# Bonus sums in column groups, later turns, and joined runs of small matmuls in a decoder layer on one core

## The chip, the cores and the metric

The kernel runs on one core of one Trainium2 chip. The metric is device time in microseconds of one execution. The kernel before takes 408.7 us, the median of three runs (408.42 to 409.23).

## What is computed

One decoder layer on 256 tokens of 1024 channels, all in float32. Two branches mix tokens from the same normalised input: RWKV-7 (a recurrence over time with a 64x64 state for each of 8 heads) and softmax attention (8 heads of 64, causal; with 256 tokens there is one key block, so the block choice picks nothing more). Both are gated and merged, projected, added to the input, and followed by a gated MLP with a short convolution. Cut to what the change touches:

```python
def step(state, inp):
    r_t, w_t, k_t, v_t, a_t, b_t = inp
    sa = jnp.einsum('bhvk,bhk->bhv', state, a_t)
    state = (state * w_t[:, :, None, :] + sa[..., None] * b_t[:, :, None, :]
             + v_t[..., None] * k_t[:, :, None, :])
    return state, jnp.einsum('bhvk,bhk->bhv', state, r_t)
...
y = ((y - mu) * lax.rsqrt(var + GN_EPS)).reshape(B, S, C)
y = y * ln_g.astype(f32) + ln_b.astype(f32)
bonus = (jnp.sum(rh * kh * r_k.astype(f32), axis=-1, keepdims=True) * vh).reshape(B, S, C)
return ((y + bonus) * g.astype(f32)).astype(z.dtype)
```

The bonus needs, for each token and head, one sum over the head's 64 channels, and that sum again at each of the 64 channels.

## The kernel before

**Projections.** Weights come from HBM in pieces of 512 KB (`load_next`, on SyncE's queue), are split by ScalarE into a high half (`split_hi`, L262) and by VectorE into a low half (`split_lo`, L272), and each product is made of three matmuls: high by high, high by low, low by high. `wst` (L300 to L305) makes blocks of 12 matmuls with 256 columns, `xst` (L321 to L325) blocks of 6 with 512 columns. These projections are the bulk of TensorE's work. The two first blocks are written out by hand in `first_steps` (L469 to L484): the first piece, its two halves (`first(0, ...)`), then the second (`first(1, ...)`), whose low half GpSimd makes (L459). Between the two stand `params_turned` (L146, a transpose of 43 rows of small parameters) and `late_params` (L150 to L152, three VectorE instructions which copy the result and derive two more vectors). Behind them comes `tl` (L490), a product with four column groups. In `first_steps` the order of every engine but SyncE is the written one (`manual_schedule`).

**The recurrence** is cut into four chunks of 64 tokens (`chain`). Within a chunk it is a triangular system. Its 64x64 matrices are inverted in levels: 16x16 blocks on the diagonal by VectorE (L722 to L750), which reach it and leave it through DRAM (`d1`, `Tb`, `d2`, `d3`, then `X0` and `X`, L695 to L772), and then two levels of small matmuls on TensorE. The first level has three products: `pp` (L836, into `P`), `px` (L850, back into `X0`) and `pxt` (L864, into `X`). `pp` and `pxt` are made for the halves h = 0 and h = 1, and the chain yields between the halves. The second level is L878 and L889. Then, per chunk c, `pz` (L943, from the second chunk on), `pu` (L952), `pS` (L963, the next state) and `pyt` (L979, L984). Before all this stand `pv` (L782), `pz0` (L793) and the group at L806 to L813: the bonus sums (L809: a 128x128 matrix `bones` with two blocks of 64x64 ones, by `bp`, the product made at L802) and the gate product (L810, L813), both in the same PSUM buffer `pb`. VectorE and ScalarE read them at L817 to L819. `pss` (L610) and `prx` (L623) are a sum with four column groups, and its spread to all channels with `spread16`, that the kernel has already for the norm of the keys.

**Group norm** (`gn`) takes each chunk's result, and ends in two transposes `pc` (L922) and four more steps. Before the transposes it yields a due time, 7.0, 5.5, 5.5 and 0.8 for the four chunks.

**Attention** (`att`) has four steps of transposes (`pqk`, L1038), three parts of scores (L1059), each followed by a softmax on VectorE and ScalarE, transposes of the weights (`ppt`, L1087) and the weighted sums (`po`, L1099).

**What sets the order.** `chain`, `gn`, `att` and `bulk` are generators. A loop at L1185 keeps a clock of its own: a generator yields a cost and a latency, and the first one in the list that is due goes on. The instructions are written down in that order; the framework then orders each engine's queue, with `tc.high_priority()` for some. `joined[0]` is true as long as the last step with a cost was not one of `bulk`. Steps of `gn` and `att` with

```python
while not joined[0] and "chain" not in done:
    yield 0, 0.1
```

wait for a step of the chain, so that they follow it in one run of small matmuls between two projection blocks. PSUM buffers come in three tags: `acc` with 3 (projections), `ch` with 3 (`chp`) and `at` with 2 (`atp`).

**Behind the generators** stands `mlp_params` (L156, a transpose of 96 rows of the MLP's parameters, and a copy), and then the RWKV branch's projection `branch(0)` (eight blocks of L300 to L305), the output projection, and the MLP (from about 220 us to the end).

## Time and profile before

| | |
|---|---|
| median of 3 runs | 408.7 us |
| profiled execution | 408.76 us |
| its span, first to last instruction | 406.9 us |
| mean granted TensorE clock | 0.998 |
| ScalarE casts of weights (L262) | 122, 1052 ns each |
| VectorE subtractions for weights (L272) | 122, 1229 ns each |
| largest group of matmuls (L1260) | 352, 395 ns each, 89.5 us busy |
| DMA, mean of the span | 173 GB/s |

A row of a timeline has the start in us, the length in us, the engine, the line, the operation, what it writes and reads, the tile of the array (rows by columns) and the shape, and a count where equal instructions are merged. In brackets stands the idle time before it, and what ended that. Matmuls overlap: the length of one (0.28 us for 256 columns) is longer than the distance to the next. So the distance between two starts is read, not the length. A matmul of two plain float32 operands shows as two records.

### The profile page before, as it was taken

How to read it: one execution, taken by the hardware profiler on the slowest of the kernel's cores; microseconds unless marked ns; L12 is line 12 of the kernel's file. 1: busy time of each engine (PE TensorE's matmuls, PEld its weight loads, DVE VectorE, ACT ScalarE, POOL GpSimd, SP SyncE). 2: the span in 40 equal slices, each digit the busy share in tenths (PEclk: the TensorE clock that was granted, in tenths of full speed). 3: DMA queues.
4: the chain of work that ended last, by engine and by line, in shares of the span. 5: the costliest groups of instructions: out<-in, count | busy, mean ns of one | idle time of the engine just before them, and what ended most of it. 6: DMA issues, size and time to landing. Idle time of an engine off the chain costs nothing.

```text
span 406.9 us, 8269 instructions
## 1 busy us (share of the span) xinstructions
PE 400.4 (98%) x3274; PEld 348.6 (86%) x3274; DVE 316.2 (78%) x537; ACT 233.0 (57%) x392; POOL 40.9 (10%) x70
## 2 busy tenths in 40 slices
PE   7999999999999999999999999999999999999996
PEld 3899899897899888999888888888888888888885
DVE  3878999769645797687975897968869778697794
ACT  6999576254655875554554864645545455365450
POOL 7810610111300010000000000000000000000000
PEclk9999999999999999999999999999999999999999
DMA  8983557644845243545564556566655666656612
GB/s 237 314 255 104 157 160 198 173 124 131 201 138 155 56 149 94 175 150 186 185 205 156 178 162 221 167 208 202 205 176 175 206 187 191 205 169 201 199 54 103
DMA packets 60191, 70.33 MB, mean 173 GB/s; under 512 B 7608, under 2 KB 50506, under 8 KB 60154
## 3 DMA queue, kind: packets, MB, share of 16 engines
q1 hardware_dynamic: 59222, 69.40, 56.2%
q0 software_dynamic: 880, 0.41, 0.5%
q8 instruction: 25, 0.41, 0.4%
q14 instruction: 12, 0.10, 0.1%
q10 hardware_dynamic: 52, 0.01, 0.0%
HBM read 68.37 MB, written 1.44 MB: 172 GB/s over the span
## 4 chain that ended last, share of the span: by engine, by line
PE 87%; DVE 6%; DMA 4%; issue 2%; POOL 1%; ACT 0%; SPq 0%; POOLq 0%; DVEq 0%
PE acc L1260 20%; PE acc L1265 10%; PE acc L300 8%; PE acc L302 7%; PE acc L305 7%; PE f L1280 4%; PE f L1282 4%; PE f L1284 4%; PE acc L321 4%; PE acc L325 3%; PE acc L322 3%; DVE wlo L272 1%; PE idle L465 1%; DMA x<-in_x_dram 1%; DMA Tb<-d 1%
## 5 line engine op out<-in xcount | busy, mean ns | idle before, releaser
L262 ACT CAST whi<-raw 128x1024 fp32r<-128x1024 f32 x122 | 127.7, 1052 | 110.8 <-PE acc L1260 41.7
L272 DVE TENSOR_TENSOR wlo<-raw,whi 128x1024 fp32r<-128x1024 f32 x122 | 149.5, 1229 | 43.6 <-PE acc L1265 12.5
L1260 PE MATMUL acc<-hx,whi 128*128 128x512 f32 x352 | 89.5, 395 | 0.0
L1260 PEld LDWEIGHTS acc<-hx,whi 128*128 128x128 f32 x352 | 63.4, 188 | 12.4
L300 PE MATMUL acc<-hx,whi 128*128 128x256 f32 x224 | 56.9, 289 | 0.0
L302 PE MATMUL acc<-hx,whi 128*128 128x256 f32 x224 | 54.6, 279 | 0.0
L1265 PEld LDWEIGHTS acc<-hx,wlo 128*128 128x128 f32 x352 | 46.8, 188 | 4.0
L1265 PE MATMUL acc<-hx,wlo 128*128 128x256 f32 x352 | 47.3, 277 | 0.0
L300 PEld LDWEIGHTS acc<-hx,whi 128*128 128x128 f32 x224 | 42.2, 188 | 2.6 <-issue 1.4
L302 PEld LDWEIGHTS acc<-hx,whi 128*128 128x128 f32 x224 | 42.2, 188 | 0.1
L305 PE MATMUL acc<-hx,wlo 128*128 128x256 f32 x224 | 34.9, 278 | 0.0
L1282 PE MATMUL f<-whi,hb 128*128 128x512 f32 x80 | 31.2, 390 | 0.0
L1284 PE MATMUL f<-wlo,hb 128*128 128x512 f32 x80 | 31.2, 390 | 0.0
L1280 PE MATMUL f<-whi,hb 128*128 128x512 f32 x80 | 31.2, 389 | 0.0
L305 PEld LDWEIGHTS acc<-hx,wlo 128*128 128x128 f32 x224 | 29.9, 189 | 0.0
L1270 DVE TENSOR_REDUCE an<-acc 128x256 f32<-128x512 f32 x22 | 14.2, 685 | 9.1 <-PE acc L1265 9.0
L321 PE MATMUL acc<-whi,hx 128*128 128x512 f32 x48 | 19.4, 405 | 0.0
L322 PE MATMUL acc<-whi,hx 128*128 128x512 f32 x48 | 18.8, 392 | 0.0
L1284 PEld LDWEIGHTS f<-wlo,hb 128*128 128x128 f32 x80 | 15.0, 188 | 3.2
L1280 PEld LDWEIGHTS f<-whi,hb 128*128 128x128 f32 x80 | 15.0, 188 | 2.8
L1282 PEld LDWEIGHTS f<-whi,hb 128*128 128x128 f32 x80 | 15.0, 188 | 2.8
L325 PE MATMUL acc<-wlo,hx 128*128 128x512 f32 x48 | 14.9, 392 | 0.0
(321 smaller groups left out, 622.0 us busy)
## 6 DMA issues: line engine op xcount, KB each, us to landing
raw<-in_w_ffn_up_dram SPq DMA_DIRECT2D x44, 512.0 KB, 4.3
raw<-in_w_in_dram SPq DMA_DIRECT2D x41, 512.0 KB, 3.9
raw<-in_w_ffn_down_dram SPq DMA_DIRECT2D x22, 512.0 KB, 3.2
raw<-in_w_out_dram SPq DMA_DIRECT2D x8, 512.0 KB, 4.2
x<-in_x_dram SPq DMA_DIRECT2D x8, 256.0 KB, 3.7
raw<-in_w_branch_b_dram SPq DMA_DIRECT2D x4, 512.0 KB, 3.5
raw<-in_w_branch_a_dram SPq DMA_DIRECT2D x4, 512.0 KB, 3.4
out_dram<-o SPq DMA_DIRECT2D x3, 256.0 KB, 2.2
```

Source lines behind the costliest of these rows:

```text
L262: act.copy(hi[:, :k * c], raw[:, :k * c])
L272: eng.tensor_tensor(lo[:, :n], raw[:, :n], hi[:, :n].bitcast(F32), op=OP.subtract)
L300: pe.matmul(om, wh[:, k, ms], xh[:, k0 + k], start=k0 + k + m == 0, stop=False, skip_group_check=True)
L302: pe.matmul(om, wh[:, k, ms], xl[:, k0 + k], start=False, stop=False, skip_group_check=True)
L305: pe.matmul(om, wl[:, k, ms], xh[:, k0 + k], start=False, stop=k0 + k == nk - 1 and m == n - 1, skip_group_check=True)
L321: pe.matmul(ps_[t], xh[:, K, ts], wh[:, k], start=K == 0, stop=False)
L322: pe.matmul(ps_[t], xl[:, K, ts], wh[:, k], start=False, stop=False)
L1260: pe.matmul(ps_[m], wh[:, k, m * 128:m * 128 + 128], hx[:, k0 + k].rearrange("p a s -> p (a s)"), start=k0 + k == 0, stop=False, skip_grou ...
L1265: pe.matmul(ps_[m][:, 0:S], wl[:, k, m * 128:m * 128 + 128], hh[:, k0 + k], start=False, stop=k0 + k == 7, skip_group_check=True)
L1280: pe.matmul(fin[f], hb[:, 0, i, ts], wh[:, 0, cs], start=st, stop=False, skip_group_check=f == 3)
L1282: pe.matmul(fin[f], hb[:, 1, i, ts], wh[:, 0, cs], start=False, stop=False, skip_group_check=f == 3)
L1284: pe.matmul(fin[f], hb[:, 0, i, ts], wl[:, 0, cs], start=False, stop=False, skip_group_check=f == 3)
```

## The change

Six edits.

1. `params_turned` and `late_params` move behind the second of the two blocks that are written out by hand.
2. The bonus sums are made with four column groups: `bp` is made one step earlier, four matmuls with every fourth column of `bones` write 32 rows each of one buffer `pbs`, ahead of `pz0`; ScalarE copies it to `bs4`; and four matmuls with `spread16` spread it over the channels, in the place of the four full sums, now behind the gate products.
3. `pp` and `pxt` no longer yield between their halves.
4. The due times before the transposes of the group norm are 10.5, 3.5, 3.5 and 0.8.
5. `mlp_params` is called in the group norm, ahead of the last chunk's transposes.
6. In the attention, the latency behind the scores is 2.5 in place of 3.0, and behind the softmax of the first two parts the generator waits until the last step was not one of `bulk`.

```diff
             first(0, 1, hh, (2, 3))
-            params_turned()
-            late_params()
             split_hi()
...
             first(1, 1, hh, (2, 3))
+            params_turned()
+            late_params()
             late_consts()
...
+            bp = zr
+            for ct in range(4):
+                dve.scalar_tensor_tensor(bp[:, ct], zr[:, ct], col(RK + ct), kp[:, ct],
+                                         op0=OP.mult, op1=OP.mult)
             yield 0.9, 4.0
+            pbs = atp("pbs")[:, 0:S]
+            for ct in range(4):
+                pe.matmul(pbs[32 * ct:32 * ct + 32], bones[:, 0:128:4], bp[:, ct], start=True, stop=True,
+                          skip_group_check=True)
+            bs4 = t1("bs4")
+            act.copy(bs4, pbs)
...
-            bp = zr
-            for ct in range(4):
-                dve.scalar_tensor_tensor(bp[:, ct], zr[:, ct], col(RK + ct), kp[:, ct],
-                                         op0=OP.mult, op1=OP.mult)
...
-                pe.matmul(pb[ct][:, 0:256], bones, bp[:, ct], start=True, stop=True, skip_group_check=True)
...
+            for ct in range(4):
+                g = slice(32 * ct, 32 * ct + 32)
+                pe.matmul(pb[ct][:, 0:256], spread16[g], bs4[g], start=True, stop=True, skip_group_check=True)
...
-                if h == 0:
-                    yield 0.6, 2.5
             P = b2("P", [128, 2, 8, 16])
...
-                if h == 0:
-                    yield 0.6, 2.5
             for h in range(2):
...
-                    yield 0, (7.0, 5.5, 5.5, 0.8)[c]
+                    yield 0, (10.5, 3.5, 3.5, 0.8)[c]
                     while not joined[0] and "chain" not in done:
                         yield 0, 0.1
+                    if c == 3:
+                        mlp_params()
...
-                yield 0.9, 3.0
+                yield 0.9, 2.5
                 softmax(*part)
+                while i < 2 and not joined[0] and "chain" not in done:
+                    yield 0, 0.1
...
-        mlp_params()
         x_sb = load_x((nc.sync, nc.sync))
```

## The prediction

> **What bounds the kernel now.** I read the page first, then the waits of TensorE, then the timeline of TensorE between 12 and 198 us, and last the chain and the timelines of the other engines where TensorE hands over to them.
>
> ```profile
> span 406.9 us, 8269 instructions
> PE 400.4 (98%) x3274; PEld 348.6 (86%) x3274; DVE 316.2 (78%) x537; ACT 233.0 (57%) x392; POOL 40.9 (10%) x70
> ...
> PE 87%; DVE 6%; DMA 4%; issue 2%; POOL 1%; ACT 0%; SPq 0%; POOLq 0%; DVEq 0%
> ```
>
> TensorE is busy for 98% of the span and holds 87% of the chain that ended last. The profiled run took 408.76 us, 1.86 us more than its span and 0.06 us more than the median of 408.7; I subtract my sum from 408.76, take the 0.06 off at the end, and let what lies around the span stay. About 0.2% (0.8 us) is what a measurement of this kernel can tell from no change.
>
> "Busy" hides small losses, so I looked at when one matmul group starts and the next one does:
>
> ```profile
> 114.81 0.62 PE L305 MATMUL acc<-hx,wlo 128*128 128x256 f32 x4
> 115.35 0.97 PE L864 MATMUL pxt<-X,P 32*16 32x16 f32 x64
> 116.25 0.66 PE L1038 MATMUL pqk<-ident,qkv 128*128 128x128 f32 x4
> 116.66 0.36 PE L300 MATMUL acc<-hx,whi 128*128 128x256 f32 x1
> ...
> 180.45 0.28 PE L300 MATMUL acc<-ybh,whi 128*128 128x256 f32 x1
> ...
> 181.81 0.28 PE L300 MATMUL acc<-ybh,whi 128*128 128x256 f32 x1
> ...
> 185.90 0.25 PE L156 MATMUL pt<-ident,p 96*128 96x96 f32 x1
> 185.93 0.36 PE L300 MATMUL acc<-yah,whi 128*128 128x256 f32 x1
> 186.13 0.28 PE L302 MATMUL acc<-yal,whi 128*128 128x256 f32 x1
> ...
> 187.43 0.28 PE L300 MATMUL acc<-yah,whi 128*128 128x256 f32 x1
> ...
> 188.84 0.28 PE L300 MATMUL acc<-yah,whi 128*128 128x256 f32 x1
> ```
>
> Three things are read here. (a) The pace: a block of 12 projection matmuls takes 181.81 - 180.45 = 1.36 us, 0.113 us each. (b) A run of small matmuls pays to get in and out: the four L305 that start at 114.81 should be through at 115.26, but the run starts at 115.35, 0.09 late. Single transposes are cheap: from 185.90 to 186.13 a transpose and one projection matmul take 0.23, so the transpose costs 0.12 with its own work. (c) There are two paces: after that transpose a block takes 188.84 - 187.43 = 1.41 us, 0.05 more, and it stays so over the eight blocks of the last branch, 0.40 us lost.
>
> **The change part by part.** TensorE carries the end, so each edit is costed as TensorE time; then comes the question whether a wait takes the time back.
>
> *Halves joined.* The second half of the inverse's first product is a run of its own now:
>
> ```profile
> 103.79 1.08 PE L836 MATMUL pp<-X,G 32*32 32x16 f32 x64
> 104.80 0.50 PE L321 MATMUL acc<-whi,hx 128*128 128x512 f32 x1
> ...
> 107.76 0.72 PE L836 MATMUL pp<-X,G 32*32 32x16 f32 x64
> 108.41 0.39 PE L300 MATMUL acc<-hx,whi 128*128 128x256 f32 x1
> 108.63 0.28 PE L302 MATMUL acc<-hx,whi 128*128 128x256 f32 x1
> ```
>
> It takes 108.41 - 107.76 = 0.65 us, and the first projection matmul behind it needs 0.22 in place of 0.113: 0.11 to get out, with 0.09 to get in 0.20 a run. Joined, the second half costs its own work alone. Whether a half's last records also wait for the array to empty, which is paid once instead of twice, no row shows; the excess at an exit, 0.11, bounds it above, 0 below. I take 0.09 for each of the two joined steps, 0.18, since the halves use the same tile size.
>
> *Runs.* I followed the planner's loop with the yields of both versions. From the inverse to the end of the two-branch part the planner before makes 20 separate small runs, and one of its transposing runs is cut by two projection matmuls, so 21: 10 end in tiled matmuls, 8 are tiled and end in a transpose or hold one inside, 3 are transposes alone. After: 17, of which 8 and 9 and none. A tiled run costs 0.20; one that leaves through transposes 0.18 by the rows at 114.81 to 116.66 and an exit like that at 186.13 (0.09); transposes alone cost nothing beside their work. So 10 x 0.20 + 8 x 0.18 = 3.44 becomes 8 x 0.20 + 9 x 0.18 = 3.22: 0.22 saved. With the joined halves 0.40, and I take 0.45, since the cut run disappears as well. Counting 4 runs at 0.20 (0.80) would be the upper bound, 0.2 the lower: the joined transposes were nearly free where they stood.
>
> *The first chunk's turn.* Only one wait of TensorE behind the first 10 us has any size:
>
> ```profile
> PE pc L922 <- DVE Sn L971: 0.5, 1, 0.5
> ...
> 149.76 0.41 DVE L971 TENSOR_TENSOR Sn<-pS,Sn 128x256 f32<-128x256 f32 x1
> ...
> 150.23 0.44 PE L922 MATMUL pc<-ident,yc 128*128 128x128 f32 x2 [0.55 <-DVE Sn L971]
> ...
> 133.38 1.13 PE L1059 MATMUL ps<-qkT,qkT 64*128 64x256 f32 x8
> ```
>
> The turn needs a PSUM buffer of the tag that the state's product holds until VectorE has read it at 150.17. The later due time puts the third score run between the two: one of its kind, at 133.38, lasts 1.13 us, more than the 0.55, so 0.55 goes. What is late next is the same buffer at the second chunk, where no wait stands today. I take -0.55; bounds 0 and -0.6.
>
> *The last transposes* (L156) go into the last run before the branches. Their work stays; the slow pace that followed them, 0.40, goes if the pace is the fast one after that run. It is so at 180.45, one block behind the last chunk's transposes. I take -0.40.
>
> *Parameters turned later.* This moves a PE transpose and three VectorE instructions behind the second weight block:
>
> ```profile
> 12.89 0.26 PE L146 MATMUL pt<-ident,p 43*128 43x43 f32 x1
> 13.08 1.19 PE L465 MATMUL idle<-hx,whi 128*128 128x256 f32 x8
> 14.11 0.65 PE L465 MATMUL idle<-hx,wlo 128*128 128x256 f32 x4
> ...
> 12.68 2.54 POOL L459 TENSOR_TENSOR wlo<-raw,whi 128x512 fp32r<-128x512 f32 x2 [0.73 <-ACT whi L454]
> ...
> 17.18 0.42 ACT L496 ACTIVATE xwa<-xwa 64x256 f32<-64x256 f32 x1 [0.55 <-DVE xwa L364]
> ...
> 19.95 1.13 PE L573 MATMUL at<-xwa,wdu 64*128 64x256 f32 x8
> ```
>
> TensorE would reach the second block 0.09 + 0.19 + 0.11 = 0.39 us earlier (in, work, out). But its low halves come from GpSimd, which has two pieces of 1.27 us to do from 12.68: the first is there at 13.95. Today the matmuls that read it start at 14.11; 0.39 earlier they would find nothing, and wait until about 14.1. So the gain is eaten, and the transpose is still to be done afterwards, ahead of a run with another tile size: 0 to 0.3 us by the row at 12.89, I take +0.15. The three VectorE instructions now stand behind a weight subtraction, and the mixing of the decay input waits for them; it has 2.35 us to spare, since its tanh ends at 17.60 and its first reader starts at 19.95.
>
> *Bonus sums.* Today four full-size sums and four gate products alternate:
>
> ```profile
> 91.16 0.59 PE L809 MATMUL pg<-zr,bones 128*128 128x256 f32 x2
> 91.59 0.59 PE L810 MATMUL pg<-xg,wgu 128*128 128x256 f32 x2
> ...
> 94.70 0.71 PE L813 MATMUL pg<-xgt,wgt 32*128 32x256 f32 x8
> 95.34 0.50 PE L321 MATMUL acc<-whi,hx 128*128 128x512 f32 x1
> 39.11 0.60 PE pss L610 x8
> ```
>
> The sums are 8 records of 0.215 (two in 0.43 us): 1.72. In their place come four sums in column groups, 0.60 (the same shape at 39.11), and four spreads of the shape of L813, 95.34 - 94.70 = 0.64. Saved: 0.48, at best 0.8, an estimate in which half of that 0.64 goes because the spread joins L813, whose shape it has. ScalarE's extra copy of 128x256 falls into a stretch where it waits.
>
> But this gain has to pass the place where the inverse begins. The run at 103.79 takes 1.01 us, its twin 0.65: it waits 0.36, and the chain says for what:
>
> ```profile
> 101.95 2.09 DMA X<-d
> ...
> 77.19 2.48 DVE L685 TENSOR_TENSOR G<-pgr,gmask 128x512 f32<-128x512 f32 x4
> ...
> 87.75 0.18 DVE L722 COPY Xb<-Tb 128x12 f32<-128x12 f32 x1 [1.89 <-DMA Tb<-d]
> ...
> 98.52 0.39 DVE L750 COPY Xb<-Xb 128x256 f32<-128x256 f32 x1
> ```
>
> The inverse's diagonal blocks land at 104.04. That chain starts with the masked products at 77.19, ahead of the bonus sums, and runs over DMAs and VectorE alone. Nothing of the edit shortens it, so TensorE comes 0.48 earlier and waits 0.48 longer. I count 0.
>
> *Sum:* -0.45 - 0.55 - 0.40 + 0.15 = -1.25 us; 408.76 - 1.25 - 0.06 = 407.45, and I say **407.4 us**. Between the bounds named it goes from -0.2 (halves and runs at the least, turn kept waiting, slow pace kept, +0 for the parameters) to -2.4 (0.8, 0.6, 0.4 and 0.6 of waits that dissolve in the new order).
>
> **The rivals.**
>
> *The slow pace stays* after the new last run. 18 blocks follow it (two of the gates, eight and eight of the branches) at 0.05 each: 0.90 lost where 0.40 is lost today, so 0.90 more than in my sum: 408.3. For it: the trace shows a pace that once entered held for eight blocks. Against: the fast block at 180.45 follows transposes closely.
>
> *The bonus gain passes*, because the new instruction order lets the inverse's VectorE part end 0.8 us earlier (it has foreign work between 87.75 and 98.52): the wait of 0.36 and the 0.48 both go, 0.84: 406.6.
>
> *Slower: the joined half is late for the next step.* The product of 103.79 is copied by ScalarE, and in the trace:
>
> ```profile
> 109.54 1.05 ACT L262 CAST whi<-raw 128x1024 fp32r<-128x1024 f32 x1 [2.47 <-DMA raw<-in_w_in_dram]
> ...
> 110.97 0.27 ACT L842 COPY P<-pp 128x128 f32<-128x128 f32 x1
> ```
>
> ScalarE stands 2.47 us for a weight load whose issue waited behind the inverse's DMAs, and the copy stands behind that. Today the next product comes behind that copy without a wait. With the halves joined (103.79 + 1.01 + 0.55, then the two projection blocks that take 107.76 - 104.80 = 2.96) TensorE gets there at about 108.3; if the copy keeps its place behind that cast, TensorE waits until 111.24, some 2.9 us: 410.3. It decides as soon as the copy's place in ScalarE's order is behind the cast. Against: the product is now done before the last value projections, so the copy should be issued ahead of it.
>
> *Nothing moves.* If TensorE's 98% were an illusion of overlapping records, shorter runs would only be filled by waiting: 408.7. Against it stands the steady 0.113 us of the blocks and the single wait row. The Trainium skill (Perfetto Trace Analysis, Identifying the Most-Contended Engine) holds matmul busy time a poor measure and weight-load busy time a good one, which is 86% here; by it TensorE would have 58 us to spare and this rival would be the forecast.
>
> **How the numbers follow.** Forecast 0.48, slow pace 0.22, bonus gain passes 0.17, late copy 0.08, nothing moves 0.05. Over 0.2% faster means under 407.9: most of the first (0.41 of 0.48), a little of the second (0.04) and the third: 0.62. Within 0.2%: the rest of the first, 0.17 of the second and the last: 0.29. Slower: the late copy and a rest: 0.09. The range leaves out the late copy and the outer ends: 406.1 (the third case with 0.5 of the waits dissolved) to 408.8 (the second with as much in new waits).
>
> **What would show it.** In the changed profile: the 32x32 product in one run of 128 records lasting 1.2 us after its wait, and that wait grown from 0.36 to about 0.8; no wait of pc on Sn; blocks of 1.36 us from 186 us on; four fewer runs between 103 and 198 us; the low-half matmuls of the second block still starting at about 14.1. I am wrong if the wait at the inverse shrinks, if new waits of TensorE over 0.5 us stand at pu, px or pc, or if the blocks of the last branch still take 1.41.

## The result, and the profile after

The changed kernel takes 412.98 us, the median of six runs (411.40 to 414.45), against 408.56 for the kernel before on the same chip (six runs, 407.94 to 409.23): a ratio of 1.0105, 95% interval 1.0081 to 1.0128. It is slower by 4.4 us. The prediction was 407.4, its range ended at 408.8, and slower had a chance of 0.09. The profiled run took 412.72 us. Of all runs below one was slow, a run of params_back (492.87 us at a granted clock of 0.754); its ratio leaves it out, and the median of the nine others is 411.25.

The page of the changed kernel hides it as well as the page before hid its small losses:

```profile
span 410.8 us, 8284 instructions
PE 400.6 (98%) x3282; PEld 349.0 (85%) x3282; DVE 315.8 (77%) x537; ACT 233.7 (57%) x393; POOL 39.7 (10%) x70
...
PE 83%; DVE 6%; DMA 4%; ACT 3%; issue 2%; POOL 2%; SPq 0%; POOLq 0%; ACTq 0%; DVEq 0%
```

TensorE is as "busy" as before, 400.6 us against 400.4. Only the chain shows a difference: its share is 83% in place of 87%. The waits of TensorE say more:

```profile
PE pc L928 <- DVE Sn L977: 1.7, 1, 1.7
...
PE pp L844 <- DMA X<-d: 1.5, 2, 0.9
...
PE idle L465 <- POOL wlo L459: 0.8, 2, 0.6
```

Three waits behind the landing of the input are new or larger. To see what each is worth, the same projection matmul is looked up in both timelines, and the two starts are subtracted:

| up to the start of | before | after | later by | in this stage |
|---|---|---|---|---|
| the first hand-written block | 9.98 | 9.66 | -0.32 | (the input's landing) |
| the first block behind `tl` | 17.91 | 18.68 | +0.77 | +1.09 |
| the block behind the bonus sums | 95.34 | 95.44 | +0.10 | -0.68 |
| the block behind `pp` | 104.80 | 107.04 | +2.24 | +2.15 |
| the last matmul of those two blocks | 107.43 | 111.08 | +3.65 | +1.41 |
| the first block of the branches | 178.98 | 182.86 | +3.88 | +0.23 |
| the last projection matmul | 403.41 | 407.36 | +3.95 | +0.07 |

The last column is taken from unrounded starts. The row of `pp` holds 0.53 us of work that has only moved up: the second half of `pp`, which was a run of 0.65 further on. The +0.23 is the 1.67 us for which `pc` waits, less that half, less the 0.55 at the first chunk, and less about 0.2 that the joined runs save.

*The start.* Here are GpSimd's and then VectorE's timeline of the changed kernel:

```profile
12.36 3.55 POOL L459 TENSOR_TENSOR wlo<-raw,whi 128x512 fp32r<-128x512 f32 x2 [0.76 <-ACT whi L454]
```
```profile
13.54 1.23 DVE L272 TENSOR_TENSOR wlo<-raw,whi 128x1024 fp32r<-128x1024 f32 x1 [0.38 <-ACT whi L262]
```

GpSimd's two pieces took 2.54 us before and take 3.55 now. In the kernel before it was VectorE's subtraction that took 2.31 us, and GpSimd's pieces were undisturbed (VectorE's timeline of the kernel before):

```profile
13.98 2.31 DVE L272 TENSOR_TENSOR wlo<-raw,whi 128x1024 fp32r<-128x1024 f32 x1
```

The three VectorE instructions that the change moved away had held VectorE's subtraction back until GpSimd's second piece had begun.

*The inverse* (TensorE's timeline, then the windows of the changed kernel and of the kernel before):

```profile
103.34 0.62 PE L325 MATMUL acc<-wlo,hx 128*128 128x512 f32 x2
104.56 0.20 PE L844 MATMUL pp<-X,G 32*32 32x16 f32 x2 [0.60 <-DMA X<-d]
105.68 1.44 PE L844 MATMUL pp<-X,G 32*32 32x16 f32 x126 [0.92 <-DMA X<-d]
107.04 0.80 PE L321 MATMUL acc<-whi,hx 128*128 128x512 f32 x1
107.64 0.63 PE L322 MATMUL acc<-whi,hx 128*128 128x512 f32 x1
```
```profile
107.00:111.40 4.40, 4.40 (x20) 3.24 (x13) 0.95 (x2) 0.91 (x3) 0.00 (x0) 0.65 1.00 288
```
```profile
107.00:111.40 4.40, 4.40 (x95) 3.85 (x94) 1.43 (x2) 1.93 (x5) 0.00 (x0) 1.00 1.02 317
```

Two waits, 0.60 and 0.92, and 1.4 us of small matmuls behind them; and then the matmuls of 512 columns go at half speed: 0.42 us from one start to the next (107.64 to 108.06) and not 0.23. The eighth column of a window is the granted clock: 0.65 where it was 1.00. The trace's clock record has it at one half from 106.67 to 110.08, 3.41 us. That is the 1.41 us of the table, and it is not the same in every run: the six runs had mean clocks of 0.999 and 0.998 (no such stretch; 411.4 and 411.7 us), 0.995 (one; 412.7 us) and 0.992, 0.990 and 0.990 (two, by 0.004 each; 413.2 to 414.5 us). Where the second one lies no trace of this kernel shows. Without any such stretch the changed kernel is still about 3 us behind.

*The second chunk* (TensorE, VectorE, GpSimd):

```profile
156.53 0.33 PE L1093 MATMUL ppt<-ident,sc 128*128 128x128 f32 x1
158.53 0.44 PE L928 MATMUL pc<-ident,yc 128*128 128x128 f32 x2 [1.67 <-DVE Sn L977]
```
```profile
154.46 1.21 DVE L272 TENSOR_TENSOR wlo<-raw,whi 128x1024 fp32r<-128x1024 f32 x1
156.58 0.43 DVE L920 TENSOR_TENSOR yc<-yc,st 128x256 f32<-128x256 f32 x1 [0.91 <-POOL st L919]
156.92 1.22 DVE L272 TENSOR_TENSOR wlo<-raw,whi 128x1024 fp32r<-128x1024 f32 x1
158.06 0.42 DVE L977 TENSOR_TENSOR Sn<-pS,Sn 128x256 f32<-128x256 f32 x1
```
```profile
154.63 1.92 POOL L919 TENSOR_TENSOR st<-st,eps 128x4 f32<-128x4 f32 x1 [15.41 <-DVE st L918]
```

The state's product (154.91, 0.69 long) is done at 155.6, and `pc` waits for the buffer until VectorE has read it, at 158.48. VectorE stands in front of that with `yc`, which waits for GpSimd's power; and that one takes 1.92 us, where it took 1.01 at this chunk before; it began during VectorE's subtraction of 154.46. In the kernel before it met none:

```profile
156.38 1.01 POOL L915 TENSOR_TENSOR st<-st,eps 128x4 f32<-128x4 f32 x1 [8.20 <-DVE st L914]
```

Behind `yc` a second subtraction (156.92) stands ahead of `Sn`. The order of VectorE's queue, not its load, makes the 1.67 us of idle time ahead of 158.53.

### The profile page after: what moved, and what is told of

Same layout as the page of the kernel before. It is cut to its first block, busy times and chain, and to the rows that moved or that the text cites. A ratio compares the mean times of both kernels' runs of the same rounds, so it can differ in the third digit from the quotient of the medians.

```text
span 410.8 us, 8284 instructions
## 1 busy us (share of the span) xinstructions
PE 400.6 (98%) x3282; PEld 349.0 (85%) x3282; DVE 315.8 (77%) x537; ACT 233.7 (57%) x393; POOL 39.7 (10%) x70
## 4 chain that ended last, share of the span: by engine, by line
PE 83%; DVE 6%; DMA 4%; ACT 3%; issue 2%; POOL 2%; SPq 0%; POOLq 0%; ACTq 0%; DVEq 0%
PE acc L1267 20%; PE acc L1272 10%; PE acc L300 7%; PE acc L302 7%; PE acc L305 7%; PE f L1289 4%; PE f L1287 4%; PE f L1291 4%; PE acc L321 4%; PE acc L325 3%; PE acc L322 3%; DVE wlo L272 2%; ACT sc L1080 1%; DMA x<-in_x_dram 1%; DMA Tb<-d 1%
## 5 line engine op out<-in xcount | busy, mean ns | idle before, releaser
L262 ACT CAST whi<-raw 128x1024 fp32r<-128x1024 f32 x122 | 127.5, 1051 | 109.4 <-PE acc L1267 41.5
L321 PE MATMUL acc<-whi,hx 128*128 128x512 f32 x48 | 20.1, 420 | 0.0
L322 PE MATMUL acc<-whi,hx 128*128 128x512 f32 x48 | 19.3, 402 | 0.0
```

The lines of the kernel that those rows point to most:

```text
L262: act.copy(hi[:, :k * c], raw[:, :k * c])
L321: pe.matmul(ps_[t], xh[:, K, ts], wh[:, k], start=K == 0, stop=False)
L322: pe.matmul(ps_[t], xl[:, K, ts], wh[:, k], start=False, stop=False)
```

## The experiments

Theory: four losses that add up (start, inverse, clock, second chunk), each made by its own edit. Rivals: the joined halves are the whole loss; or the late start is, and the rest follows from it. Seventeen kernels ran, five rounds each; ratios are to the kernel before on the same chip.

| kernel | median, us | ratio, 95% interval |
|---|---|---|
| params_back | 411.44 | 1.0066, 1.0042 to 1.0089 |
| c1_later | 409.97 | 1.0029, 1.0008 to 1.0050 |
| pp_late | 410.34 | 1.0035, 1.0014 to 1.0055 |
| filled | 412.50 | 1.0106, 1.0066 to 1.0146 |
| filled_c1 | 410.65 | 1.0047, 1.0030 to 1.0063 |
| halves_split | 409.82 | 1.0023, 1.0006 to 1.0039 |
| dve_order_only | 409.59 | 1.0011, 0.9998 to 1.0025 |
| bonus_only | 409.23 | 1.0012, 0.9994 to 1.0030 |
| joined_only | 408.46 | 0.9994, 0.9977 to 1.0011 |
| halves_only | 411.57 | 1.0070, 1.0057 to 1.0083 |
| halves_joined_c1 | 408.58 | 1.0008, 0.9995 to 1.0020 |
| pp_join_only | 411.21 | 1.0052, 1.0033 to 1.0070 |
| pxt_join_only | 411.13 | 1.0055, 1.0036 to 1.0074 |
| pp_join_late | 409.16 | 1.0016, 1.0003 to 1.0029 |
| late_joined_bonus | 408.86 | 1.0011, 1.0000 to 1.0021 |
| pp_join_late_runs | 409.60 | 1.0028, 1.0008 to 1.0048 |
| pp_join_late_all | 409.09 | 1.0007, 0.9990 to 1.0024 |

### Parts of the changed kernel undone

**params_back**: the start as before.

```diff
             first(0, 1, hh, (2, 3))
+            params_turned()
+            late_params()
...
             first(1, 1, hh, (2, 3))
-            params_turned()
-            late_params()
```

> The changed kernel with its first edit undone: the turned parameters and the three VectorE instructions stand between the two first blocks again. Theory (four losses that add up: about 1.1 us at the start, where VectorE's first weight subtraction now runs beside GpSimd's low half and stretches it from 1.29 to 2.29 us; about 1.7 us more of waiting at the inverse's first product; 1.4 us for each half-speed window of the clock behind that wait; 2.0 us at the second chunk's transposes): the GpSimd pieces take about 1.3 us each again, the wait for them at the second block shrinks from 0.6 to about 0, everything behind comes 0.8 to 1.1 us earlier, the wait at the inverse stays near 2 us since its VectorE part comes earlier by the same amount; about 1.0 us under the changed kernel, 411 to 412. Rival (the start only shifts what the inverse waits for anyway): no difference, 412.7 to 413. Rival (the start is the whole loss and the rest follows from it): back to 408.5.

411.44: the theory's number. From the first hand-written block to the one behind `tl` it takes 7.98 us, as before the change (7.93), against 9.02 in the changed kernel. And something showed that nobody had expected: `px` runs in two pieces (TensorE's timeline, then the page of that line and of the DMA that it reads):

```profile
108.68 0.23 PE L856 MATMUL px<-P,X 32*32 32x16 f32 x2
109.51 0.72 PE L856 MATMUL px<-P,X 32*32 32x16 f32 x62 [0.60 <-issue]
```
```profile
L856 PEldq EVENT_SEMAPHORE  x2: 51/1685/3319, 105.6 to 106.1; - x2
```
```profile
DMA to landing us min/median/max: 1.9/2.1/5.4
```

"Issue" stands for idle time in which the profile shows nothing that the engine waited for. It isn't the whole truth here: a semaphore wait in the queue of the weight loads lasts from 106.1 for 3.32 us, to 109.4, and one of the eight transfers of the diagonal blocks into `X` took 5.4 us to land, which fits; it was not tried by itself. In the kernel before such a transfer takes 5.0 us too, but `px` starts at 111.34 there. The joined run brought TensorE to it 2.7 us earlier.

**c1_later**: one number.

```diff
-                    yield 0, (10.5, 3.5, 3.5, 0.8)[c]
+                    yield 0, (10.5, 5.5, 3.5, 0.8)[c]
```

> The changed kernel with one number altered: the second chunk's due time before its transposes is 5.5 as before the change, and not 3.5. By the planner's loop the transposes then stand in the next run, behind the fourth chunk's pz, and not in the run of the state's product. Theory: the stall of 2.0 us of pc on Sn at 156.5 us goes, and no other wait of that size takes its place; 1.5 to 2.0 us under the changed kernel, 410.5 to 411.5. Rival (VectorE and GpSimd are late for this chunk whatever the order, so that the stall moves to the next place where pc or pz stands): within 0.5 of the changed kernel, with a wait of over 1 us at pz, pu or pc.

409.97, under the expected range: the wait of `pc` is gone and none of its size has come in its place. The ratio falls by 0.0076, some 3 us, which is more than the 1.67 us of that wait. Part of it may be the clock: none of the 12 runs is under 0.996 (one half-speed stretch), while three of six runs of the changed kernel are at 0.990 to 0.992. That the second stretch followed the wait of `pc` is argued and not shown. The profiled run is a piece of luck for the start as well. It has the changed kernel's order there, and GpSimd was first by 0.2 us (GpSimd, then VectorE):

```profile
11.82 2.54 POOL L459 TENSOR_TENSOR wlo<-raw,whi 128x512 fp32r<-128x512 f32 x2 [0.21 <-ACT whi L454]
```
```profile
13.32 2.12 DVE L272 TENSOR_TENSOR wlo<-raw,whi 128x1024 fp32r<-128x1024 f32 x1 [0.69 <-ACT whi L262]
```

GpSimd's second piece began at 13.08; its two pieces take 2.54, and VectorE's subtraction 2.12. From the first block to the one behind `tl` it takes 8.11 us, only 0.18 more than before the change. With the change the start has become a race.

**pp_late**: `yield 0, 5.5` ahead of `pp` becomes `yield 0, 8.5`.

> The changed kernel with the due time ahead of the inverse's first product 8.5 and not 5.5: two more projection blocks of 1.3 us stand ahead of it, which come from behind it. Theory: TensorE reaches the product at about 106.5 us, when the diagonal blocks have landed (105.5), so the wait of 2.1 us goes, and with it the half-speed window (granted clock at least 0.998 in all runs, no stretch under 1.00 between 100 and 200 us); 2.5 to 3.5 us under the changed kernel's 412.7 and a spread between runs under 1 us: 409.2 to 410.2. Rival (the half-speed window has another cause than this wait): the wait goes, the window stays at some place behind it: about 411. Rival (the wait is a resource's, not a place's, and moves to px): a wait of over 1 us at px, 412.

The wait at `pp` is gone and the time is 410.34, just above the expected range; but `px` now waits 1.3 us and `pxt` 0.5 on "issue", and 4 of 12 runs have a mean clock of 0.996. The rival of a wait that moves to `px` is half true. What that "issue" is comes further down.

**filled** and **filled_c1**: ten matmuls whose result nothing reads, and the same with c1_later's number.

```diff
             yield 0, 5.5
+            fl = chp("fill")
+            for _ in range(10):
+                pe.matmul(fl, rst[:, 0:128], rst[:, 0:512], start=True, stop=True)
```

> The changed kernel with ten matmuls more, 128x512 with 16-bit operands, right ahead of the inverse's first product; their result is read by nothing. They take about 2.1 us, about as long as TensorE waits there now. Theory: the product starts when the data are there or some tenths later, so the time up to its end is the same or 0.4 us longer, but TensorE isn't idle, so the half-speed window behind it goes: granted clock at least 0.998 in all runs, 1.0 to 1.4 us under the profiled run of the changed kernel and up to 2.5 under its slowest runs, median 411.3 to 412. Rival (the half-speed windows have nothing to do with this wait): clocks of 0.990 to 0.995 stay in most runs, and the median is 0 to 0.5 us above 413.

> The changed kernel with ten matmuls more ahead of the inverse's first product (their result is read by nothing) and with the second chunk's due time at 5.5. Theory (each half-speed window follows from a stretch in which TensorE waits for about 2 us out of 3.4): with the wait at the inverse filled and the one at the second chunk gone, no run has a half-speed window: clock at least 0.998 in all, and the spread between runs is as small as that of the kernel before. The time is that of the changed kernel with the due time alone without its windows, 409 to 410, as what is waited for at the inverse is still waited for. Rival (the windows have another cause): 0.996 in some 4 of 12 runs.

Mean clocks of 0.996 in 2 of 6 and 2 of 10 runs, against 4 of 6 with 0.990 to 0.995 in the changed kernel and 6 of 12 with 0.996 in c1_later. With the wait filled the half-speed stretches seem rarer, though the runs are few, and the theory's "none" is wrong: another wait in the same stretch, at `px`, stays. The times (412.5 and 410.65) gain nothing, as what TensorE waits for is still waited for.

**halves_split**: `if h == 0: yield 0.6, 2.5` is back in both products.

> The changed kernel with its third edit undone: both products of the inverse's first level again in two runs. Theory: joining gains 0.2 us a run and loses 0.6 us at px, where TensorE waits for instructions: a joined run uses up 256 of them in 1.2 us, and they come in blocks of 16 KB over a DMA queue, here behind weight loads. So no wait of px on issue, but two more runs; the wait at the inverse's first half stays at 1.5 to 2.1 us with half-speed windows in some runs; in the order that the planner's loop gives for it, the second chunk's transposes stand behind eight transposes of the attention, so that their wait for Sn is under 1.2 us. 411 to 412.3. Rival (the joined halves are the cause of the slowdown): 408.3 to 409.3.

409.82, some 3 us under the changed kernel and nearer to the rival's range than to the theory's: most of the loss hangs on the third edit. The wait at `pp` (1.2) and the one at the start (0.5) are there; the wait of `pc` is gone altogether, since `pc` now stands behind eight transposes.

### One edit alone on the kernel before

**dve_order_only**: `late_params()` behind `split_lo()`; the transpose stays.

> The kernel before with one thing altered: the three VectorE instructions on the turned parameters stand behind VectorE's first weight subtraction, as in the changed kernel; TensorE's transpose stays where it was. Theory (a VectorE weight subtraction and a GpSimd low half don't run side by side: the one that starts second lasts until about 1.0 us after the first has ended): the two now start within 0.3 us of each other; where VectorE is first, GpSimd's piece takes 2.3 us and not 1.3, TensorE waits 0.6 to 1.0 us for it and all behind it is as late; where GpSimd is first, nothing is lost. So runs between 0 and 1.0 us above the kernel before, median 408.9 to 409.7. Rival (it is the transpose's place on TensorE that costs at the start): 408.5 to 408.7, and GpSimd's pieces take 1.3 us each.

0.7 us slower in the medians (409.59 and 408.90), though the interval of the ratio just holds 1. What decides is the trace: GpSimd, VectorE and TensorE:

```profile
12.72 3.51 POOL L459 TENSOR_TENSOR wlo<-raw,whi 128x512 fp32r<-128x512 f32 x2 [0.75 <-ACT whi L454]
```
```profile
13.62 1.47 DVE L272 TENSOR_TENSOR wlo<-raw,whi 128x1024 fp32r<-128x1024 f32 x1
```
```profile
16.29 0.72 PE L465 MATMUL idle<-hx,wlo 128*128 128x256 f32 x4 [0.52 <-POOL wlo L459]
```

Nothing was moved on TensorE, and it waits as in the changed kernel. From the first block to the one behind `tl` it takes 8.78 us against 7.93, so 0.85 of the 1.09 lost at the start comes from the order of the two subtractions. The rest fits the transpose's place: filled_c1, whose subtractions take as long as here (1.48 and 2.28) but whose transpose has moved, needs 8.99, 0.2 more.

**bonus_only**: the second edit.

> The kernel before with the second edit alone (bonus sums in column groups). Theory (the sums save 0.68 us, but all of it and more is waited for at the inverse's first product, since the new order of VectorE's and SyncE's instructions lets the diagonal blocks land some 0.5 us later): the wait there grows from 0.36 to about 1.5 us, the landing from 104.0 to about 104.5; 408.7 to 409.4. Rival (the later landing in the changed kernel came from its late start alone): the wait is about 1.0, the landing at 104.0, the time that of before. Rival (the gain passes): 408.0.

```profile
104.39 0.70 PE L844 MATMUL pp<-X,G 32*32 32x16 f32 x62 [1.06 <-DMA X<-d]
105.02 0.50 PE L321 MATMUL acc<-whi,hx 128*128 128x512 f32 x1
```

The sums save 0.68 us. The half at `pp` lasts from 103.09 to 105.02, 1.93, of which 0.65 is work: it waits 1.28 where it waited 0.36. So the 0.68 is waited for, and 0.24 more, since the blocks land later; up to the block behind `px` another 0.5 is lost, 0.2 of it to a wait for the copy of `P`. 0.3 us slower in the medians, within the interval.

**joined_only**: the fourth to sixth edits.

> The kernel before with the due times, the MLP's parameters in the last run and the attention's shorter latency and wait, and nothing else. Theory: the wait of 0.55 us at the first chunk goes and some runs fall away, but the transposes of the second chunk (due time 3.5) wait for VectorE's Sn, which stands behind yc and a weight subtraction, for 1 to 2 us; and 264 matmuls behind the last run go at 0.118 us and not 0.113 (1.0 us lost where 0.4 was). The wait at the inverse stays 0.36, the clock stays 1.0 in all runs. 409.0 to 410.0. Rival (the second chunk's wait in the changed kernel came from everything being later, and not from these edits): 407.6 to 408.2.

The rival is right about the mechanism: there is no wait at `pc`. The time, 408.46 against 408.90, lies a little above its range, and the interval holds 1. The second chunk's short due time is harmless with these pairings (the steps of the chain, the group norm and the attention that share a run). It is not the cause by itself.

**halves_only**, and **pp_join_only** and **pxt_join_only** with one of the two products joined:

> The kernel before with the third edit alone (both halves of the inverse's first level in one run each). Theory (joining itself saves 0.4 us of TensorE, but TensorE then waits 0.5 to 0.8 us at px for its next 256 instructions; the rest of what it costs in the changed kernel comes from the runs behind it, which the planner's loop pairs in another way with the attention): a wait of px on issue, the wait at pp 0.36, the clock 1.0 in all runs; the transposes of the first chunk stand in a run by the loop just ahead of the second chunk's state product and wait for nothing, those of the second behind the state's product and wait for Sn. 408.7 to 410. Rival (joining halves is harmless without the short due time of the second chunk): 408.0 to 408.7, without a wait at pc. Rival (joining halves costs 3 us by itself): over 411.

> The kernel before with only the first product of the inverse's first level (pp) in one run, pxt in two. Theory: in the trace TensorE stops inside runs of small matmuls at the same count of its instructions (193 or 194 behind a multiple of 256) and goes on 1.3 to 1.6 us after a 16 KB packet of its instruction queue: the joined runs use up instructions faster than that queue, behind weight loads, brings them. With pxt in two runs the second packet has three more projection blocks' time, so no wait of pxt on issue; px comes 3.6 us earlier than before, at about 108.2, while the last diagonal block lands at about 109: a wait of 0 to 0.8 us there, so far hidden. No half-speed window. 408.4 to 409.8. Rival (the broken order of the later runs costs the 3 us): 410.5 or more, with waits at pc, po or pS and none at pxt.

> The kernel before with only the last product of the inverse's first level (pxt) in one run, pp in two. The planner's loop gives the same order behind pxt as where pp alone is joined. Theory (instructions come too late): one run of 128 records comes two projection blocks behind px, and asks for its second 256 instructions some 2.9 us later than where both are joined, so a wait of pxt on issue of 0 to 0.5 us; px as before the change. 408.2 to 409.3. Rival (a joined run costs by itself): the wait on issue is there with 1.1 us as where both are joined, and half-speed windows behind it in some runs; over 410. Rival (the order behind costs it): the same time as where pp alone is joined, over 410.

Joining both products, and nothing else, costs 3 us; joining either one costs 2.3, the same for both. halves_only has the wait on issue, at `pxt`, and behind it a half-speed stretch (TensorE, and a window of it with the granted clock in the eighth column):

```profile
111.77 1.14 PE L862 MATMUL pxt<-X,P 32*16 32x16 f32 x84
114.04 0.72 PE L862 MATMUL pxt<-X,P 32*16 32x16 f32 x44 [1.13 <-issue]
```
```profile
115.30:118.80 3.50, 3.50 (x19) 3.50 (x18) 0.00 (x0) 1.72 (x4) 0.00 (x0) 0.51 0.32 110
```

In halves_only `pc` waits only 0.31 us, and the four runs of six that show no half-speed stretch (clock 1.0) still take 410.3 to 411.7 us. The wait of 1.13 covers part of that; where the rest goes is open. The two kernels with one product joined have neither the wait nor the stretch at `pxt`. The joined runs themselves are cheaper (TensorE, first of pxt_join_only, then of pp_join_only):

```profile
115.21 1.69 PE L864 MATMUL pxt<-X,P 32*16 32x16 f32 x128
116.84 0.66 PE L1036 MATMUL pqk<-ident,qkv 128*128 128x128 f32 x4
```
```profile
111.44 0.97 PE L862 MATMUL pxt<-X,P 32*16 32x16 f32 x64
112.34 0.65 PE L1036 MATMUL pqk<-ident,qkv 128*128 128x128 f32 x4
```

116.84 - 115.21 = 1.63 in one run, 2 x 0.90 in two: 0.17 saved. The loss stands further on (the waits of pxt_join_only, and VectorE's timeline):

```profile
PE pc L920 <- DVE Sn L969: 1.6, 1, 1.6
```
```profile
146.00 1.23 DVE L1075 TENSOR_TENSOR sc<-sc,sm 128x1024 f32<-128x1024 f32 x1
147.14 1.21 DVE L1068 TENSOR_REDUCE mx<-sc 128x4 f32<-128x1024 f32 x1
148.27 0.41 DVE L969 TENSOR_TENSOR Sn<-pS,Sn 128x256 f32<-128x256 f32 x1
```

By the planner's loop a missing yield brings all the later steps of the chain one place forward against the attention. `pc` now meets a VectorE that has two softmax instructions in front of `Sn`, and the attention's transposes cut a projection block in two. In pp_join_only `pc` waits as long, 1.65 us. The order behind is the same in both kernels, and so is the loss; the rival that put it down to the pairings was right. The sizes fit: in both, the waits at `pc`, `ppt` and `pS` together grow by 1.7 us, and the runs with a clock of at least 0.998 have medians 1.9 and 1.4 us above the kernel before. The rest of the 2.3 is the clock: 4 runs of 8 and 4 of 10 are at 0.994 to 0.996, and pp_join_only's trace has it at one half from 149.21 to 152.62, right behind `pc`, which started at 148.49. In the changed kernel the wait shows at the second chunk.

**halves_joined_c1**: the third to sixth edits with c1_later's number.

> The kernel before with the third to sixth edits and the second chunk's due time left at 5.5: neither the start nor the bonus sums are changed. Theory: the wait at the inverse is 0.36 or less, no half-speed window in any run; px waits 0.5 to 0.8 us for instructions, which eats the 0.4 of the joined halves; the joined runs bring 0.2 to 0.7: 408.0 to 408.9. Rival (the joined halves bring a wait somewhere else, whatever the start and the bonus sums): over 409.5, with a wait of over 1 us at pc, pz or pu.

408.58: with other due times the pairings are harmless, and the joined halves cost nothing, but bring nothing either. There is a wait on issue again, at `pxt` (0.4 us) and not at `px`, and one run of 11 has a clock of 0.994 and takes 411.1 us, which the theory excluded. So the wait of `pc` in the changed kernel needs both: without the joined halves (joined_only, halves_split) or without the short due time (c1_later, halves_joined_c1) it is not there.

### A joined run with the pairings of before

**pp_join_late**: `pp` in one run, at the place of its second half (due time 8.5).

> The kernel before with pp joined at the place of its second half: the due time ahead of it is 8.5 and not 5.5. By the planner's loop everything behind it, and every pairing with the attention, is as in the kernel before. Theory (joining costs nothing by itself; the 2 to 3 us come from the pairings behind, which the missing yield shifts): pp finds its blocks landed, so the wait of 0.36 us goes, and the joined run saves 0.12; px waits for nothing; no wait of pc beside the 0.55 of before: 0.4 to 0.5 us under the kernel before, ratio 0.9988 to 0.9992. Rival (a joined run costs by itself): 410 or more.

It should have been 0.4 us faster, and is 0.3 to 0.7 slower. The order behind is that of before, and `pp` waits for nothing, but:

```profile
106.28 1.26 PE L836 MATMUL pp<-X,G 32*32 32x16 f32 x128
110.50 0.36 PE L848 MATMUL px<-P,X 32*32 32x16 f32 x20
111.67 0.55 PE L848 MATMUL px<-P,X 32*32 32x16 f32 x44 [0.81 <-issue]
```

No semaphore is waited for at `px` here. What is short is instructions. The page lists a queue of its own for them:

```profile
q8 instruction: 25, 0.41, 0.4%
```

These are 25 packets of 16 KB. TensorE's 6588 records (matmuls, weight loads and the waits among them) make 25.7 times 256; and from the packet at 137.5 us to the one at 378.1, 13 packets move while 3325 records start, 256 to a packet. So a packet holds 256 of them. The trace shows when each packet moved and at which count of its instructions TensorE stopped: at 1985 here, in pp_join_late_runs and in pp_join_late_all, at 1985 and 2241 in pp_late, 1986 in filled_c1, 2242 in halves_only and halves_joined_c1. All these counts lie 193 or 194 above a multiple of 256, and each stop ends 1.3 to 1.6 us after a packet of that queue (here 109.1 to 110.2, then 111.67). Weight loads fill the DMA engines at that time (busy share 1.0 to 1.1 from 106 to 111.7 us). Two small runs with a projection block between use a packet up slowly; a joined run of 128 records uses 256 instructions in 1.2 us.

**late_joined_bonus** (the second, fourth, fifth and sixth edits, one block more ahead of `pp`), **pp_join_late_runs** and **pp_join_late_all** were tries at a faster kernel.

> The kernel before with the second, fourth, fifth and sixth edits, and the due time ahead of the inverse 7.0 and not 5.5, which by the planner's loop puts one projection block more ahead of the first product; start and halves as before the change. Theory: the bonus sums' 0.68 us passes, as TensorE now reaches the product at 104.2, 0.3 us ahead of the landing; the joined runs bring their 0.2 to 0.7; one projection block and not two between the second half and px leaves less room for the copy of P: a new wait of 0 to 1.3 us there. 407.5 to 408.8. Rival (the chain is the limit, so that a later start makes each later step wait): over 409.5.

> The same with the fourth to sixth edits, whose pairings behind pp are by the loop those that they have without joined halves. Theory: the two gains add up, 0.4 to 0.5 and 0.2 to 0.7: 407.7 to 408.3, no wait of TensorE over 0.3 us between 100 and 180 us. Rival (one gain eats the other): 408.3 to 408.9.

> The same with the second edit too (bonus sums in column groups); of the change, only the first edit and the joined pxt are left out. Theory: the 0.68 us saved by the sums is no longer waited for at pp, which stands 1.6 us behind the landing; px comes 1.2 us earlier than before the change, at about 110.9, and may wait up to 0.5 us for the copy of P, which ScalarE makes behind a cast that waits for a weight load: 407.2 to 407.9, the fastest of all. Rival (the copy of P and the last diagonal block hold px back by all of it): 408 to 408.5.

All three miss: `px` waits 1.0 and 1.1 us for instructions in the last two, and in the first the gain at `pp` is spent on new waits and split runs behind. None is faster than the kernel before; joined_only, with a ratio of 0.9994, can't be told from it.

## Why the prediction was wrong

- **Halves joined**, -0.18: right as a local price (0.12 for `pp`, 1.31 to 1.19, and 0.17 for `pxt`), and the step that failed most. "Joined, the second half costs its own work alone" leaves out that a yield is also the planner's clock and a pause for the instruction queue. Joined alone: +3.0 us (halves_only) in place of -0.2. Behind the joined `pp`, `px` meets a transfer (0.6 us in params_back) or an instruction packet (0.8 in pp_join_late) that had been hidden, and by the missing yields `pc` meets a late `Sn` (1.67 us in the changed kernel).
- **Runs**: 18 and not 17. The 8 and 9 tiled runs are as counted, but the run that two projection matmuls cut is still cut (163.08, and its last four transposes at 165.43), so the 0.05 taken for that did not come. In joined_only the runs, the first chunk's turn and the last transposes together (-0.27, -0.55 and -0.40 in the sum) bring 0.44 us in the medians. Its trace is 0.65 us ahead behind the first chunk and 0.23 at the branches; 0.22 of what it gives back lies at that cut, whose two projection matmuls last 0.58 in place of 0.36. I counted the runs of the new order and not what each would meet on the other engines.
- **First chunk's turn**, -0.55: the wait did go (0.07 us of idle time is left). "What is late next is the same buffer at the second chunk, where no wait stands today": the place was named and not priced; TensorE stands idle there for 1.67 us.
- **The slow pace**: this rival came true. All 216 projection matmuls of 256 columns behind the last run go at 0.118 us, and the -0.40 is not there. What sets the pace is open. The order doesn't: joined_only and halves_split have the same one behind the last chunk's transposes, and their blocks start (joined_only, then halves_split) at

```profile
181.65 0.28 PE L300 MATMUL acc<-ybh,whi 128*128 128x256 f32 x1
...
183.01 0.28 PE L300 MATMUL acc<-ybh,whi 128*128 128x256 f32 x1
```
```profile
182.63 0.28 PE L300 MATMUL acc<-ybh,whi 128*128 128x256 f32 x1
...
184.04 0.28 PE L300 MATMUL acc<-ybh,whi 128*128 128x256 f32 x1
```

  1.36 us a block in one and 1.41 in the other.
- **Parameters turned later**, +0.15: as the price of the transpose's new place this was about right (0.2). But I took GpSimd's piece as 1.27 us whatever VectorE does, while the row beside it, 2.31 for a subtraction that takes 1.23 elsewhere, showed that the two don't run side by side. It is +0.85 more where VectorE is first, 1.09 in all.
- **Bonus sums**, 0: the saving is 0.68 (I said 0.48, at best 0.8), and it is waited for, as said; the wait takes 0.2 more than it gives.
- **The clock** is in no part of the prediction. Its 1.4 us come with the growing wait that I did forecast.
- Of the rivals, the late copy of `P` didn't happen: it was made at 107.12. Of the signs named for being wrong, two came: a new wait at `pc`, and blocks of 1.41 us in the last branch. The wait at the inverse grew, as forecast, but to 1.5 us and not to 0.8.

By edits, against the kernel before: start 0.11% (dve_order_only, without the transpose), bonus 0.12%, halves 0.70%, the rest -0.06%; together 0.87% of the 1.05% measured. That this comes near is in part luck. Undone one at a time in the changed kernel, the start takes off 0.39%, the second chunk's due time 0.76% and the halves 0.82%, together far more than 1.05%: the losses overlap, and halves_only loses its time at other places than the changed kernel. How much of the whole belongs to each edit stays open; that most of it goes with the third edit and the pairings it makes is shown.

## What to carry to other kernels

A yield in a hand-planned order is a price, a place and a pause. Taking one out moves everything behind it, so the new order has to be walked through with the other engines' queues in hand, above all the first instruction of each that releases a buffer. A wait that a profile doesn't show is not a wait that can't appear: one transfer into `X` landed 5.0 us after its issue in the kernel before too, and a packet of the instruction queue took about 1 us there as well; both were covered by work that the change moved away. And a gain in front of a gate should be priced with the gate's own inputs, and with what a longer wait does to the clock.

## What the runs showed of the hardware

- A VectorE subtraction and a GpSimd one, each with two operands in SBUF, exclude each other. The one that begins second takes about 1.0 us longer (GpSimd 1.29 to 2.27 or 2.29, VectorE 1.23 to 2.31), and a difference of 0.1 us in their starts decides which. The Trainium skill (SBUF — State Buffer, "SBUF: two separate sides") states this as a lock held for a whole instruction by the one that starts first; the traces here agree.
- The clock halves for 3.41 us after stretches in which TensorE is not idle throughout: waits of 0.60 and 0.92 with 1.4 us of small matmuls in the changed kernel, 1.13 with some 1.6 us of them in halves_only (0.51 granted from 115.30 to 118.80). In the 3.41 us ahead of the fall TensorE was busy for 1.89 us in the changed kernel, 2.28 in halves_only and 1.76 in pp_join_only. The Trainium skill (TensorE: Matmul & The Clock Gate, "What's actually happening") has the length, 3413 ns, and a window that runs freely, which agrees with runs of one kernel that have none, one or two; its demand for a whole idle window is not what these runs show. Under 0.998 were one of 141 runs of the kernel before (0.949, in the round of pp_join_late), one of 11 of bonus_only (which waits 1.3 us at `pp`), and 5 of 12 of halves_split. What the threshold is, and whether small matmuls count as less, no run shows.
- The Trainium skill (Runtime: NRT & Kernel Launch, "Instruction fetch mechanics") has the 16 KB blocks of 256 instructions, and calls the cost of crossing one mostly hidden. Here it was 0.4 to 1.3 us in eight stops in seven kernels, each in or behind a joined run. Not every joined run stops: `pxt` of the changed kernel and of pxt_join_only does not. That weight loads delay the packets is argued from the full DMA engines; no run took them away.
